# Conditioning sums in fixed runs, more load buffers and split row statistics in the first stage of a diffusion backbone kernel

## The chip, the core and the metric

The kernel runs on one core of a Trainium2 chip. A core has TensorE (PE in the profile, with its weight loads as PEld), VectorE (DVE), ScalarE (ACT), GpSimd (POOL) and SyncE (SP), and sixteen DMA engines that move data between memory and the on-chip buffers. Every engine works through its own list of instructions in order and waits at semaphores for the others. All loads of this kernel are issued from SP. The metric is the time of one execution on the device, in microseconds (us); a change is measured against runs of the kernel before.

## The reference

Two layers of a diffusion backbone over 256 latent tokens and 256 context tokens of width 2048, all in float32. Only the part that the first stage computes is shown: shift and scale from the conditioning vectors, the normed and modulated tokens, and the first products with the input projection.

```python
def rms_norm(x, g):
    xf = x.astype(jnp.float32)
    y = xf * lax.rsqrt(jnp.mean(xf * xf, axis=-1, keepdims=True) + EPS)
    return (y * g.astype(jnp.float32)).astype(x.dtype)

def modulate(h, shift, scale):
    return h * (1.0 + scale[:, None, :]) + shift[:, None, :]

def ada_mods(cvec, w, b):
    m = jax.nn.silu(cvec) @ w + b
    return jnp.split(m, N_MOD, axis=-1)
...
        sh1, sc1, gt1, sh2, sc2, gt2 = ada_mods(c, w_ada[layer], b_ada[layer])
        hl = modulate(rms_norm(x, g_norm_mix[layer]), sh1, sc1)
        hc = None
        if ctx_read:
            csh1, csc1, cgt1, csh2, csc2, cgt2 = ada_mods(c_ctx_row, w_ada[layer], b_ada[layer])
            hc = modulate(rms_norm(ctx_s, g_norm_mix[layer]), csh1, csc1)
        if layer % 2 == 0:
            e = layer // 2
            yl, yc = even_mixer(hl, hc, w_in_even[e], w_out_even[e], lbs[0, e], lbs[1, e], g_hgrn_out[e],
                                w_spatial[e], b_spatial[e], g_spatial_v[e], ctx_out_needed)
```

After the mixer (gated linear attention heads beside chunk MLP heads, an output projection, a residual) each layer has a squared-ReLU MLP; layer 1 has a pooling mixer. The change leaves all of that as it is.

## The kernel before, in words

Weights come as raw float32 chunks of up to 1 MB into two buffers of tag raw (`load_w`, lines 172 to 188), and are cut into two parts that TensorE multiplies fast: hi by a cast on ScalarE (line 183), lo by a subtraction on VectorE (line 184), each in three buffers. Tokens are cut in the same way into `xt`.

The first stage is `startup`. It loads the 256 latent and 256 context rows as four blocks of 128 rows (`xraw`), takes the sum of squares of each block in four pieces on ScalarE (line 460), makes all four row factors in one GpSimd instruction (`rstd`, line 289), and scales the blocks by eight VectorE instructions (line 467). Then it goes through nine slices of features, two of one tile of 128 features (numbers 0 and 1) and seven of two tiles (2 to 8). For each slice it

- sums the conditioning weights over all 2048 features (`cond`, lines 477 to 491): tiles `sraw` of 512 KB, two for each of the slice's `2 * nk` pieces, four buffers of tag a4 in all, are multiplied as plain float32 with the conditioning vectors (`cst`, 32 columns) into `ps_as`. Feature tile kt goes to column group kt mod 4 of TensorE, so four tiles in a row use the four groups. A matmul of plain float32 leaves two records in the profile, so one `sraw` tile of a two-tile slice shows as x4;
- copies the sums to `sp`, adds up the four groups with small matmuls (`ps_ac`), transposes the tokens (`ps_t`), applies scale and shift and cuts the result (`modulate`);
- multiplies the tokens with its rows of two weights: `values` (`mmi`, two calls, summed in `v`) and `forgets` (`mmf`, three calls for three heads, summed in `fbacc`).

`cond` and `modulate` of slice i + 1 are written between the five calls of slice i. A scheduler with priorities and its own clock sets the order on each engine, and where two lists are ready it may interleave them; `issue_after` forces an instruction behind another.

After the stage come eight attention heads with the remaining input projections. There and in what follows VectorE also sums up the other conditioning vectors in the background (`ada_task`, lines 295 to 321): 320 tiles `araw` of 512 KB, one multiply-add each (line 310), in the same four a4 buffers, of which one holds the running sum `acc`.

Of the kernel before, what the change touches and what calls it, by code (L numbers as in the profile page):

```python
# [12 lines left out]
F32 = mybir.dt.float32  # L13
# [6 lines left out]
P = 128  # L20
D = 2048
KT = D // P
T = 256
# [12 lines left out]
BATCH = 2  # L36
NG4 = 7
# [3 lines left out]
AT_S = 1  # L41
# [23 lines left out]
def _cols(v):  # L65
    """(..., n * 128) -> (128, ..., n): one value per partition."""
# [84 lines left out]
class Builder:  # L151
    def __init__(self, nc, tc, I, out):
# [4 lines left out]
        self.n_raw = 0  # L157
        self.hold, self.norm = [], None
# [65 lines left out]
    def group_a(self, chunks, lhs, blocks=(0, 1), cols=512):  # L224
        """lhs(kt, blk) -> (hi, lo) [128, 128]; returns psum tiles of two blocks each, or of one if narrow."""
# [23 lines left out]
    def rows_out(self, src, c0, lhs, narrow):  # L249
        """K = 2048 and all 2048 columns in groups of 512, the last ones narrow if asked; yields (psum, first column, width)."""  # L250
# [10 lines left out]
    def group_b(self, chunks, xt):  # L261
        """psum[:, n, 0] holds W_hi x_lo, psum[:, n, 1] holds W_hi x_hi + W_lo x_hi."""
# [12 lines left out]
    def sum_b(self, ps, out):  # L275
        """out [128, 2, 256] = the two halves of group_b."""
# [15 lines left out]
    def ada_task(self, task, dst, row):  # L292
        """task: 1024 columns of w_ada; dst: [128, 8] columns, or a list for a broadcast row."""
# [805 lines left out]
```

## Time and profile before

| what | value |
|---|---|
| median of 3 runs | 2315.47 us (2312.16 to 2319.08) |
| the profiled execution, span | 2316.0 us |
| TensorE busy | 2262.3 us (98%) |
| VectorE busy | 1683.7 us (73%) |
| ScalarE busy | 1101.6 us (48%) |
| first stage, to the last slice's first matmul | 201.6 us |
| data moved | 582.72 MB, mean 252 GB/s |

The page of the profile gives busy time by engine, the chain of work that ended last and the costliest groups of instructions. A busy TensorE is not one at its best: a matmul that keeps only part of the array at work counts as busy as well. So the stages are read one by one from a table of windows, and inside a window from the instructions in order of time. The waits of an engine name who released it last.

### The profile page before, as it was taken

Reading aid. Unit: us, or ns where it says so; the run is one execution under the profiler, and the core shown is the slowest. Engines: PE = TensorE matmul, PEld = TensorE weight load, DVE = VectorE, ACT = ScalarE, POOL = GpSimd, SP = SyncE. Lnnn points to the kernel's source line nnn. Section 1 sums busy time; section 2 is a strip of 40 time slices with the busy share of each in tenths; the row PEclk is TensorE's granted clock in tenths of the full one; section 3 lists DMA queues with packets and bytes.
Section 4 is the critical chain, followed back from the end, with each engine's and each line's share of the span. In section 5 each row is a group of like instructions: output and inputs, shape, how many; then the busy total and the mean of one; then the engine's idle time right before and its main releaser. Section 6 shows DMA issues by size and latency. Waiting matters only on the chain.

```text
span 2316.0 us, 31681 instructions
## 1 busy us (share of the span) xinstructions
PE 2262.3 (98%) x12486; PEld 1855.1 (80%) x12486; DVE 1683.7 (73%) x2038; ACT 1101.6 (48%) x1493; POOL 34.6 (1%) x43
## 2 busy tenths in 40 slices
PE   6999999999999999999999999999999999999998
PEld 3557778778878888888887888888888888888887
DVE  3447989898878766777879888859875555656655
ACT  4224546464535544553554554545444443443443
POOL 0000000001000000000000000000000000000000
PEclk9999999999999999999999999999999999999999
DMA  8576676777878777888878888755875555555553
GB/s 300 213 271 236 220 263 246 252 257 285 300 289 291 283 282 258 291 303 309 302 289 318 308 318 308 264 177 210 294 283 209 186 196 190 185 188 191 191 183 126
DMA packets 111357, 582.72 MB, mean 252 GB/s; under 512 B 13012, under 2 KB 13140, under 8 KB 67304
## 3 DMA queue, kind: packets, MB, share of 16 engines
q1 hardware_dynamic: 111208, 580.70, 69.7%
q8 instruction: 98, 1.61, 0.3%
q14 instruction: 51, 0.42, 0.0%
HBM read 578.55 MB, written 2.10 MB: 251 GB/s over the span
## 4 chain that ended last, share of the span: by engine, by line
PE 80%; DVE 7%; DMA 6%; issue 5%; ACT 2%; POOL 0%; DVEq 0%; SPq 0%; POOLq 0%; ACTq 0%
PE mma L220 34%; PE mmb L220 32%; PE mmf L220 4%; DMA araw<-in_wada 4%; PE mmn L220 3%; PE ps_as L220 2%; PE mmi L220 2%; DVE acc L310 2%; DVE lo L184 2%; ACT hi L183 1%; DMA raw<-in_w_out 1%; PE ps_ada L220 1%; DVE kk L700 0%; PE ps_t L220 0%; ACT junk L460 0%
## 5 line engine op out<-in xcount | busy, mean ns | idle before, releaser
L183 ACT CAST hi<-raw 128x1024 fp32r<-128x1024 f32 (+1 forms) x701 | 731.9, 1046 | 931.7 <-PE mma L220 430.3
L184 DVE TENSOR_TENSOR lo<-raw,hi 128x1024 fp32r<-128x1024 f32 (+1 forms) x701 | 848.2, 1214 | 381.4 <-ACT hi L183 380.1
L220 PE MATMUL mma<-hi,xt 128*128 128x512 f32 x2800 | 872.5, 390 | 0.1
L220 PE MATMUL mmb<-xt,hi 128*128 128x512 f32 x2304 | 814.6, 398 | 1.1 <-DVE xt L388 0.8
L220 PE MATMUL mmb<-xt,lo 128*128 128x256 f32 x2304 | 647.9, 281 | 1.8 <-DVE lo L184 1.8
L220 PEld LDWEIGHTS mma<-hi,xt 128*128 128x128 f32 x2800 | 524.7, 188 | 111.8 <-issue 0.6
L220 PE MATMUL mma<-lo,xt 128*128 128x512 f32 x1400 | 547.2, 391 | 3.6 <-DVE lo L184 3.6
L220 PEld LDWEIGHTS mmb<-xt,hi 128*128 128x128 f32 x2304 | 432.7, 188 | 105.9 <-DVE xt L388 1.0
L310 DVE SCALAR_TENSOR_TENSOR acc<-araw,csil,acc 128x1024 f32<-128x1024 f32 x320 | 409.5, 1280 | 91.7 <-DMA araw<-in_wada 90.3
L220 PEld LDWEIGHTS mmb<-xt,lo 128*128 128x128 f32 x2304 | 435.3, 189 | 4.7 <-DVE lo L184 2.7
L220 PEld LDWEIGHTS mma<-lo,xt 128*128 128x128 f32 x1400 | 262.9, 188 | 62.6 <-DVE lo L184 7.3
L220 PE MATMUL mmf<-xt,hi 128*128 128x512 f32 x512 | 164.6, 394 | 0.0
L220 PEld LDWEIGHTS mmf<-xt,hi 128*128 128x128 f32 x512 | 95.6, 188 | 26.7 <-issue 7.1
L220 PE MATMUL mmf<-xt,lo 128*128 128x512 f32 x256 | 101.0, 395 | 0.0
L220 PE MATMUL mmn<-hi,xt 128*128 128x256 f32 x416 | 76.0, 283 | 0.0
L220 PE MATMUL ps_as<-sraw,cst 128*32 128x512 f32 (+1 forms) x288 | 58.2, 600 | 18.0 <-DMA sraw<-in_wada_h 17.8
L220 PEld LDWEIGHTS mmn<-hi,xt 128*128 128x128 f32 x416 | 65.2, 192 | 0.4
L220 PEld LDWEIGHTS mmf<-xt,lo 128*128 128x128 f32 x256 | 48.1, 188 | 14.5 <-issue 5.0
L220 PE MATMUL mmn<-lo,xt 128*128 128x256 f32 x208 | 58.8, 283 | 0.0
L540 DVE TENSOR_TENSOR v<-mmi,v 128x1024 f32<-128x1024 f32 x16 | 19.6, 1223 | 50.5 <-PE mmi L220 50.5
L388 DVE TENSOR_TENSOR xt<-hup,xt 128x512 fp32r<-128x512 f32 x64 | 43.9, 686 | 12.2 <-ACT xt L387 12.2
L220 PE MATMUL mmi<-hi,xt 128*128 128x512 f32 x128 | 48.4, 432 | 2.5 <-ACT xt L518 2.4
(178 smaller groups left out, 1318.6 us busy)
## 6 DMA issues: line engine op xcount, KB each, us to landing
araw<-in_wada SPq DMA_DIRECT2D x320, 512.0 KB
raw<-in_w_up SPq DMA_DIRECT2D x128, 1024.0 KB
raw<-in_w_down SPq DMA_DIRECT2D x128, 1024.0 KB
sraw<-in_wada_s SPq DMA_DIRECT2D x56, 512.0 KB
raw<-in_w_out SPq DMA_DIRECT2D x16, 1024.0 KB
raw<-in_w_pool SPq DMA_DIRECT2D x16, 1024.0 KB
raw<-in_w_fb SPq DMA_DIRECT2D x10, 1024.0 KB
raw<-in_w_q SPq DMA_DIRECT2D x8, 1024.0 KB
```

The costliest lines, as they stand in the source:

```text
L183: nc.scalar.copy(hi, raw[:, o:o + w])
L184: nc.vector.tensor_sub(lo, raw[:, o:o + w], hi.bitcast(F32))
L220: self.first_mm = self.nc.tensor.matmul(out, lhsT, rhs, start=start, stop=stop, **kw).ins
L310: nc.vector.scalar_tensor_tensor(acc, raw, self.csil[:, c, 0:1], acc, ALU.mult, ALU.add)
L388: return self.nc.vector.tensor_sub(x[:, :, lo], src, x[:, :, hi].bitcast(F32))
L540: nc.vector.tensor_add(dst, ps, dst)
```

## The change

`cond` is called twice for a slice, each time for half of its pieces: four `sraw` tiles in a two-tile slice, two in a one-tile slice. The last tile is multiplied first, and all other matmuls of the run are tied behind that one. The five calls of a slice and the pieces of the next one are tied in a fixed order: values 0, cond run 0, values 1, cond run 1, forgets 0, modulate, forgets 1 and 2. The tag a4 has seven buffers instead of four, for the background's `araw` too, and `sraw` has two more of its own (tag s4, in a pool that lives only as long as `startup`). [...] Squares and scaling of blocks 1 and 3 go to VectorE, those of 0 and 2 stay with or go to ScalarE; each block gets a row factor of its own. Comments were taken out too, so line numbers differ.

```diff
+NA4 = 7
+NS4 = 2
...
-AT_S = 1
...
-        stat = self.tp.tile([P, 4], F32, tag="st4", bufs=1, name="stat4")
+
+        r4 = [self.tp.tile([P, 1], F32, tag="r4", bufs=4, name="r4") for _ in range(4)]
         for b in range(4):
...
-                nc.scalar.activation(junk, xs[b][j // 2][:, 512 * (j % 2):512 * (j % 2) + 512], AF.Square, accum_out=acc2[:, j:j + 1])
-            nc.vector.tensor_reduce(stat[:, b:b + 1], acc2, AX.X, ALU.add)
-        nc.vector.tensor_scalar(stat, stat, 1.0 / D, EPS, ALU.mult, ALU.add)
-        r4 = self.tp.tile([P, 4], F32, tag="r4", bufs=1, name="r4")
-        self.rstd(stat, r4, 4)
-        for b in range(4):
-            for z in xs[b]:
-                nc.vector.tensor_scalar(z, z, r4[:, b:b + 1], None, ALU.mult)
+                z = xs[b][j // 2][:, 512 * (j % 2):512 * (j % 2) + 512]
+                if b % 2:
+                    nc.vector.scalar_tensor_tensor(junk, z, 1.0, z, ALU.mult, ALU.mult, accum_out=acc2[:, j:j + 1])
+                else:
+                    nc.scalar.activation(junk, z, AF.Square, accum_out=acc2[:, j:j + 1])
+            ms = self.tp.tile([P, 1], F32, tag="ms4", bufs=4, name="ms4")
+            nc.vector.tensor_reduce(ms, acc2, AX.X, ALU.add)
+            nc.vector.tensor_scalar(ms, ms, 1.0 / D, EPS, ALU.mult, ALU.add)
+            self.rstd(ms, r4[b], 1)
+        for j in range(2):
+            for b in range(4):
+                z = xs[b][j]
+                if b % 2:
+                    nc.vector.tensor_scalar(z, z, r4[b], None, ALU.mult)
+                else:
+                    nc.scalar.activation(z, z, AF.Copy, scale=r4[b])
...
-        def cond(i, c):
+        def cond(i, run):
...
+            for c in range(run * nk, run * nk + nk):
+                src = I["wada_h"][2 * k0 + c] if nk == 1 else I["wada_s"][2 * k0 - 4 + c]
+                for h in range(2):
+                    self.n_sraw += 1
+                    if self.n_sraw % (NA4 + NS4) < NS4:
+                        t = self.sp.tile([P, 1024], F32, tag="s4", bufs=NS4, name="sraw")
+                    else:
+                        t = self.ap.tile([P, 1024], F32, tag="a4", bufs=NA4, name="sraw")
+                    nc.sync.dma_start(t, src[:, 1024 * h:1024 * h + 1024])
+                    todo += [(n * c + j, t, j * w % 1024) for j in range(n) if j * w // 1024 == h]
+            first = None
+            for kt, t, at in todo[::-1]:
...
+                with self.tc.issue_after(first) if first is not None else nullcontext():
+                    m = self.mm(st["psa"][32 * g:32 * g + 32, 0:w], cst[:, kt, :], t[:, at:at + w], start, run == 1 and kt < n * nk + 4, skip_group_check=True)
+                first = first if first is not None else m
...
+            steps = [lambda: values(i, 0, wi[0])] + more * [lambda: cond(i + 1, 0)] + [lambda: values(i, 1, wi[0])]
+            steps += more * [lambda: cond(i + 1, 1)] + [lambda: forgets(i, 0, wf)] + more * [lambda: modulate_first(i + 1)]
+            steps += [lambda h=h: forgets(i, h, wf) for h in range(1, N_START)]
+            for fn in steps:
+                with self.tc.issue_after(st["last"]) if "last" in st else nullcontext():
+                    fn()
+                st["last"] = self.first_mm
...
-    nc = bacc.Bacc("TRN2", target_bir_lowering=False, num_devices=1)
+    nc = bacc.Bacc("TRN2", target_bir_lowering=False, num_devices=1, dynamic_dma_scratch_size=1024)
```

TensorE, where slice 3's values are multiplied (`mmi<-hi,xt_96`), in the kernel before; `ps_as x2` is one `sraw` tile for slice 4:

```order
L220 MATMUL ps_as<-sraw,cst 32x512 x2
L220 MATMUL mmi<-hi,xt_96 128x512
L220 MATMUL mmi<-lo,xt_96 128x512
L220 MATMUL mmi<-hi,xt_96 128x512
L220 MATMUL ps_as<-sraw,cst 32x512 x2
L220 MATMUL mmi<-hi,xt_96 128x512
L220 MATMUL mmi<-lo,xt_96 128x512
L220 MATMUL mmi<-hi,xt_96 128x512 x2
```

The same place in the changed kernel, from the end of values 0 on:

```order
L222 MATMUL mmi<-hi,xt_96 128x512
L222 MATMUL ps_as<-sraw,cst 32x512 x8
L222 MATMUL mmi<-hi,xt_96 128x512
L222 MATMUL mmi<-lo,xt_96 128x512
L222 MATMUL mmi<-hi,xt_96 128x512 x2
```

The tiles of slice 4 no longer stand one by one between single matmuls; the four of a run are together, and a second run of x8 stands behind values 1.

ScalarE, from the end of slice 1 to slice 2, in the kernel before (`xt1` holds the tokens of slice 2, `hi<-raw 128x1024` and `128x512` the weights):

```order
L495 COPY sp_425<-ps_as_360 128x512
L183 CAST hi_466<-raw_464 128x1024
L515 ACTIVATE mtmp_441<-ps_t_436,mcol_432 128x256
L518 CAST xt1_95<-mtmp_441 128x512
L183 CAST hi_472<-raw_470 128x1024
L183 CAST hi_476<-raw_470 128x512
L515 ACTIVATE mtmp_451<-ps_t_446,mcol_432 128x256
L518 CAST xt1_95<-mtmp_451 128x512
```

The same place in the changed kernel, with the last copies of slice 0's `forgets` and slice 1's tokens `xt0` ahead:

```order
L575 COPY fbacc_198<-mmf_344 128x1024
L538 ACTIVATE mtmp_339<-ps_t_334,mcol_330 128x256
L575 COPY fbacc_199<-mmf_352 128x1024
L541 CAST xt0_94<-mtmp_339 128x512
L185 CAST hi_478<-raw_476 128x1024
L518 COPY sp_429<-ps_as_380 128x512
L185 CAST hi_484<-raw_482 128x1024
L185 CAST hi_488<-raw_482 128x512
L538 ACTIVATE mtmp_445<-ps_t_440,mcol_436 128x256
L541 CAST xt1_95<-mtmp_445 128x512
```

Both casts of the `forgets` weights of slice 2 now stand ahead of the first `mtmp` of slice 2; and the third copy of slice 0 stands ahead of the cast of slice 1's tokens.

VectorE, around the start of slice 8 (`xt7` holds its tokens), in the kernel before:

```order
L519 TENSOR_TENSOR xt7_101<-mtmp_1335,xt7_101 128x2x256
L519 TENSOR_TENSOR xt7_101<-mtmp_1345,xt7_101 128x2x256
L310 SCALAR_TENSOR_TENSOR acc_1475<-araw_1478,csil_78,acc_1475 128x1024
L554 TENSOR_TENSOR fbacc_186<-mmf_1305,fbacc_186 128x1024
L184 TENSOR_TENSOR lo_1373<-raw_1370,hi_1372 128x1024
L184 TENSOR_TENSOR lo_1377<-raw_1370,hi_1376 128x512
L554 TENSOR_TENSOR fbacc_187<-mmf_1350,fbacc_187 128x1024
```

The same place in the changed kernel:

```order
L312 SCALAR_TENSOR_TENSOR acc_1491<-araw_1497,csil_78,acc_1491 128x1024
L526 TENSOR_TENSOR mcol_1324<-ps_ac_1319,bcol_213 128x4 x2
L577 TENSOR_TENSOR fbacc_197<-mmf_1303,fbacc_197 128x1024
L527 SCALAR_TENSOR_TENSOR mcol_1324<-mcol_1324,gcol_215 128x4
L312 SCALAR_TENSOR_TENSOR acc_1491<-araw_1500,csil_78,acc_1491 128x1024
L540 TENSOR_SCALAR mtmp_1333<-ps_t_1328,mcol_1324 128x256
L540 TENSOR_SCALAR mtmp_1343<-ps_t_1338,mcol_1324 128x256
L577 TENSOR_TENSOR fbacc_198<-mmf_1348,fbacc_198 128x1024
L542 TENSOR_TENSOR xt7_101<-mtmp_1333,xt7_101 128x2x256
L542 TENSOR_TENSOR xt7_101<-mtmp_1343,xt7_101 128x2x256
L312 SCALAR_TENSOR_TENSOR acc_1491<-araw_1545,csil_78,acc_1491 128x1024
```

The first tiles of the background (`acc<-araw`) moved up: three of them now stand ahead of slice 8's tokens, where none stood. Counted from there on, about four more of them stand ahead of a given weight cut than before all through the heads.

## Rows read from the trace of the kernel before

**Rows 1.** Page: busy time, share of the span and instructions of each engine.

```profile
PE 2262.3 (98%) x12486; PEld 1855.1 (80%) x12486; DVE 1683.7 (73%) x2038; ACT 1101.6 (48%) x1493; POOL 34.6 (1%) x43
```

**Rows 2.** Windows: length, busy PE, PEld, DVE, ACT, POOL; granted clock, DMA share, GB/s.

```profile
0.00:27.76 27.76, 7.31 (x49) 2.61 (x49) 9.80 (x28) 15.66 (x41) 2.33 (x11) 1.00 0.92 337
...
40.95:58.98 18.03, 16.29 (x75) 7.77 (x71) 8.54 (x12) 3.13 (x6) 0.00 (x0) 1.00 0.86 305
58.98:85.76 26.78, 26.78 (x109) 14.06 (x109) 11.35 (x17) 7.13 (x11) 0.00 (x0) 0.94 0.58 207
85.76:110.72 24.96, 24.96 (x109) 13.51 (x108) 12.00 (x17) 5.26 (x8) 0.00 (x0) 1.00 0.61 222
110.72:134.49 23.77, 23.77 (x109) 13.46 (x108) 11.50 (x16) 5.26 (x8) 0.00 (x0) 1.00 0.69 254
134.49:156.80 22.31, 22.31 (x110) 13.59 (x109) 11.58 (x16) 5.36 (x8) 0.00 (x0) 1.00 0.68 248
...
179.12:201.60 22.48, 22.30 (x109) 13.77 (x109) 12.59 (x17) 5.31 (x8) 0.95 (x1) 1.00 0.68 251
201.60:560.00 358.40, 343.95 (x2582) 278.41 (x2581) 325.16 (x618) 202.72 (x379) 10.33 (x8) 1.00 0.70 251
```

**Rows 3.** PE in order of time, three places: start, duration, instruction [wait before].

```profile
39.63 0.39 PE L220 MATMUL mmf<-xt,hi 128*128 128x512 f32 x1
39.95 1.07 PE L220 MATMUL ps_as<-sraw,cst 128*32 128x512 f32 x8
...
41.28 0.39 PE L220 MATMUL mmi<-lo,xt 128*128 128x512 f32 x1
...
85.44 0.39 PE L220 MATMUL mmf<-xt,hi 128*128 128x512 f32 x1
85.76 1.05 PE L220 MATMUL ps_as<-sraw,cst 128*32 128x512 f32 x4
...
87.08 0.39 PE L220 MATMUL mmi<-lo,xt 128*128 128x512 f32 x1
87.31 0.40 PE L220 MATMUL mmi<-hi,xt 128*128 128x512 f32 x1
...
178.80 0.39 PE L220 MATMUL mmf<-xt,hi 128*128 128x512 f32 x1
179.12 1.92 PE L220 MATMUL ps_as<-sraw,cst 128*32 128x512 f32 x16
...
181.31 0.40 PE L220 MATMUL mmi<-lo,xt 128*128 128x512 f32 x1
```

**Rows 4.** SP's waits, 0 to 201.6 us: total, times, longest.

```profile
SPq L485 <- PE ps_as L220: 115.3, 47, 9.4
```

**Rows 5.** Windows as in rows 2: a slow stretch, and a fast one for DMA.

```profile
60.00:64.00 4.00, 4.00 (x12) 1.68 (x10) 2.33 (x3) 1.48 (x3) 0.00 (x0) 0.64 0.00 0
...
1250.00:1300.00 50.00, 50.00 (x255) 41.28 (x254) 44.87 (x42) 22.52 (x26) 0.95 (x1) 1.00 0.89 321
```

**Rows 6.** The head in order of time: DVE's scaling, PE's last load wait.

```profile
17.80 5.39 DVE L467 TENSOR_SCALAR xraw<-xraw,r 128x1024 f32<-128x1024 f32 x8 [1.22 <-POOL r L289]
...
21.04 1.08 PE L220 MATMUL ps_as<-sraw,cst 128*32 128x256 f32 x8 [0.15 <-DMA sraw<-in_wada_h]
```

**Rows 7.** ACT and PE in order of time at the ends of slices 0 and 1.

```profile
40.30 1.02 ACT L552 COPY fbacc<-mmf 128x1024 f32<-128x1024 f32 x1
...
58.83 1.56 ACT L183 CAST hi<-raw 128x1024 fp32r<-128x1024 f32 x2
...
58.98 0.50 PE L220 MATMUL mmi<-hi,xt 128*128 128x512 f32 x1 [1.49 <-ACT xt L518]
```

**Rows 8.** DVE in order of time around the start of slice 8.

```profile
198.68 1.28 DVE L310 SCALAR_TENSOR_TENSOR acc<-araw,csil,acc 128x1024 f32<-128x1024 f32 x1
...
203.27 1.22 DVE L554 TENSOR_TENSOR fbacc<-mmf,fbacc 128x1024 f32<-128x1024 f32 x1
```

**Rows 9.** DVE's waits, 201.6 to 560 us: total, times, longest.

```profile
DVE acc L310 <- DMA araw<-in_wada: 15.7, 12, 3.0
```

More of the change, by code (lines that the diff above doesn't have):

```diff
@@ L297, in first @@
         def first():
-            st["acc"] = self.ap.tile([P, 1024], F32, tag="a4", bufs=4, name="acc")
+            st["acc"] = self.ap.tile([P, 1024], F32, tag="a4", bufs=NA4, name="acc")
             nc.gpsimd.memset(st["acc"], 0.0)
@@ L304, in chunk @@
                 first()
-            raw = self.ap.tile([P, 1024], F32, tag="a4", bufs=4, name="araw")
+            raw = self.ap.tile([P, 1024], F32, tag="a4", bufs=NA4, name="araw")
             nc.sync.dma_start(raw, self.I["wada"][task * 16 + c])
@@ L314, in last @@
         def last():
-            hi, lo = (self.ap.tile([P, 1024], F32R, tag="a4", bufs=4, name="apart") for _ in range(2))
+            hi, lo = (self.ap.tile([P, 1024], F32R, tag="a4", bufs=NA4, name="apart") for _ in range(2))
             nc.scalar.copy(hi, st["acc"])
@@ L474, in startup @@
         slices = [(0, 1), (1, 1)] + [(k, 2) for k in range(2, KT, 2)]
-        def cond(i, c):
+        def cond(i, run):
             k0, nk = slices[i]
-            n_c, w = 2 * nk, 256 * nk
-            if c == 0:
-                st["psa"] = self.pa.tile([P, 512], F32, tag="ax", name="ps_as")
-            src = I["wada_h"][2 * k0 + c] if nk == 1 else I["wada_s"][2 * k0 - 4 + c]
-            raws = [self.ap.tile([P, 1024], F32, tag="a4", bufs=4, name="sraw") for _ in range(2)]
-            for h in range(2):
-                nc.sync.dma_start(raws[h], src[:, 1024 * h:1024 * h + 1024])
-            n = 2048 // w
-            for j in range(n):
-                at = j * w % 1024
-                g, kt = j % 4, n * c + j
-                self.mm(st["psa"][32 * g:32 * g + 32, 0:w], cst[:, kt, :], raws[j * w // 1024][:, at:at + w], kt < 4, kt >= KT - 4, skip_group_check=True)
+            w = 256 * nk
+            n = 2048 // w
+            if run == 0:
+                st["psa"], st["seen"] = self.pa.tile([P, 512], F32, tag="ax", name="ps_as"), set()
+            todo = []
+            for c in range(run * nk, run * nk + nk):
[10 more added lines that the diff above has]
+            for kt, t, at in todo[::-1]:
+                g = kt % 4
+                start = g not in st["seen"]
+                st["seen"].add(g)
+                with self.tc.issue_after(first) if first is not None else nullcontext():
+                    m = self.mm(st["psa"][32 * g:32 * g + 32, 0:w], cst[:, kt, :], t[:, at:at + w], start, run == 1 and kt < n * nk + 4, skip_group_check=True)
+                first = first if first is not None else m
         def modulate(i):
@@ L565, in startup @@
             wf = self.load_w(I["w_fbs"][k0 // 2, :, n * j:n * (j + nk)], n * nk)
-            ahead = []
-            if i + 1 < len(slices):
-                ahead = [lambda c=c: cond(i + 1, c) for c in range(2 * slices[i + 1][1])] + [lambda: modulate_first(i + 1)]
-            todo = [lambda w=w: values(i, w, wi[0]) for w in range(2)] + [lambda h=h: forgets(i, h, wf) for h in range(N_START)]
-            for q, fn in enumerate(todo):
-                if ahead and q == len(todo) - AT_S:
-                    ahead.pop()()
-                elif q < 2:
-                    for _ in range((len(ahead) - 1) // (2 - q)):
-                        ahead.pop(0)()
-                fn()
+            more = i + 1 < len(slices)
+            steps = [lambda: values(i, 0, wi[0])] + more * [lambda: cond(i + 1, 0)] + [lambda: values(i, 1, wi[0])]
[5 more added lines that the diff above has]
+                st["last"] = self.first_mm
         return fbacc
@@ L805, in gmlp_u, with mixer_even @@
         self.split(4 + pair, 2, 3, u)
-    def mixer_even(self):
+    def mixer_even(self, fbacc):
         nc, I = self.nc, self.I
-        fbacc, fbs = self.startup(), {}
+        fbs = {}
         self.plan(LEFT_H, LOADS_H)
@@ L1054, in build @@
             self.NG4, self.NT2 = NG4, NT2
[L1055 removed]
+            with pool(name="tp0", bufs=1) as self.tp, pool(name="vp", bufs=1) as self.vp:
                 self.ada(1, c["sh2_0"])
@@ L1065, in build @@
                 gate2 = self.ada(9, None)
-                self.mixer_even()
-                stat = self.out_proj()
+                with pool(name="sp", bufs=1) as self.sp:
+                    fbacc = self.startup()
+                with pool(name="gp", bufs=1) as self.gp:
+                    self.mixer_even(fbacc)
+                    stat = self.out_proj()
             with pool(name="gates", bufs=4) as self.gate_pool:
```

4 lines of the change are left out of this document (2 added, 2 removed).

## The prediction

> **What bounds the kernel now.** I read the busy times first: TensorE is busy 98% of the span [rows 1], so whatever makes the kernel shorter must either make TensorE's own work shorter or fill its idle 54 us. Next I read the table of windows, cut at the slices of the first stage [rows 2]. The reader should see three things. In the first 27.76 us TensorE does little and DMA moves 337 GB/s: the head is loading. From 58.98 us on TensorE has no idle time, yet slices 2 to 5, which do the same work, take 26.78, 24.96, 23.77 and 22.31 us; slices 6 and 7 are like 5. So busy TensorE time differs in length, and DMA is used to 58 to 69% only. In the heads (201.6 to 560 us) TensorE idles 358.40 - 343.95 = 14.45 us and VectorE is busy 91%.
>
> Why the slices differ is in the instructions in order of time [rows 3]. An undisturbed matmul starts 0.23 us after the last (87.08 to 87.31). Where a single `sraw` tile stands between two matmuls (x4), the second matmul behind it starts 87.08 - 85.44 = 1.64 us after the one ahead, instead of 2 x 0.23: the tile costs **1.18 us**. Two tiles together (x8) cost 41.28 - 39.63 - 0.46 = **1.19 us**, no more than one, since they fill all four column groups where one fills two. Four tiles (x16) cost 181.31 - 178.80 - 0.46 = **2.05 us**. In TensorE's order slices 2 and 3 have eight single tiles (8 x 1.18 = 9.44 us), slices 1 and 4 one x8 and six singles (8.27), slices 5 to 7 one x16 and four singles (6.77). This accounts for the table: slice 3 less slice 5 should be 2.67 and is 2.65 us, slice 4 less slice 5 should be 1.50 and is 1.46.
>
> **Runs of four tiles.** After the change each slice from 1 to 7 has two x16: 4.10 us, and nothing stands inside them. Slices 2 and 3 gain 5.34 us each, slice 4 4.17, slices 5 to 7 2.67 each: 22.9 us together, and a slice should take 22.31 - 2.67 = 19.6 us. Slice 1 gains 4.17 too. [...]
>
> [...]
>
> **Loads.** A waiting run holds up TensorE, as the run now starts with its last tile. Today SP waits 115.3 us in the stage for TensorE to free an `sraw` buffer [rows 4]; with nine buffers the next slice's tiles can be issued one slice ahead, right after the run that frees them. A slice moves eight tiles of 512 KB, 512 KB and 768 KB of weights, 5.5 MB. In 19.6 us that is 280 GB/s; the best stretch later in the trace keeps 321 GB/s [rows 5], the head 337 [rows 2], by which 5.5 MB need 17.1 us. So some 2.5 us of each slice are spare and I charge nothing. What stands in SP's list ahead of the tiles is the `forgets` weight load, which waits for a raw buffer until its predecessor has been cut, early in a slice; what it holds up is needed a slice later. If this cover is gone, the loads set the pace: a rival below. Slices 1 and 2 have the least reserve, since all nine buffers must first be filled behind the head; a wait of 0 to 3 us may fall there.
>
> **The order on ScalarE between slices 0, 1 and 2** is worse. Today slice 2's first matmul waits 1.49 us for its tokens on ScalarE [rows 7], of 18.03 - 16.29 = 1.74 us idle in slice 1 [rows 2]. Afterwards both casts of the `forgets` weights (1.56 us, [rows 7]) stand ahead of these tokens, and the second can only start when slice 1's last matmul has freed its buffer. I take 1.49 + 1.56, some 3.0 us, which is 1.3 more than now; bounds 0 and 3 more than now. At the end of slice 0 the third copy (1.02 us, [rows 7]) now stands between the last `forgets` and the cast of slice 1's tokens, where nothing waits today: 1.02 plus the cast and its way, bounded by the 1.49 of the other place, 1.0 to 2.5; I take 2.0. [...]
>
> **Row statistics.** Today the squares run on ScalarE alone and scaling takes VectorE 5.39 us, until 23.19 us [rows 6]. In halves, with a row factor per block, I see the scaling end up to 2 us earlier, worked out from VectorE's list: it waits for block 0's squares, does block 1's (four pieces, half of a 1.28 us operation each), waits for GpSimd, and the same again for blocks 2 and 3. But slice 0's sums wait for loads: the last tile comes at 21.04 us [rows 6], and afterwards a run starts with it, so that up to 1.08 us of matmuls move behind it; ScalarE also casts a weight before it copies the sums. I take 0; bounds -1.5 and +1.5.
>
> **Slice 8.** VectorE now has three background operations ahead of slice 8's tokens and a fourth behind them (its order is shown above), where one stood in all. At 1.28 us each [rows 8] the sum `fbacc`, for whose buffer `values` 1 of slice 8 waits, which began at 203.27, 1.67 us after the slice [rows 8], comes up to 3.8 us later. Some of that is in VectorE's spare time: +2.5 us, bounds 0 and 4.
>
> **The heads.** The background has seven buffers, so its tiles land earlier. VectorE waits 15.7 us for them in the heads [rows 9] and TensorE idles 14.45 us there [rows 2]. Only some of these idle times follow such a wait, and the scheduler puts about four background operations earlier, ahead of work that TensorE waits for. I take -2 us; bounds -12 (nearly all idle time gone) and +8 (an operation of 1.28 us ahead of a wait in six of the eight heads). Behind 560 us nothing is charged: TensorE has few gaps there, and VectorE has room for work that comes earlier. [...]
>
> **The sum.** -22.9 (slices 2 to 7), -4.2 + 1.3 (slice 1), -0.5 + 2.0 (slice 0), 0 (head), +2.5 (slice 8), -2 (heads): -23.8 us. The profiled execution has a span of 2316.0 us, 0.5 above the median of the runs; 2315.5 - 23.8 gives **2292 us**. Its own bounds, with the larger terms not all at one end together, are 2283 to 2303.
>
> **The rivals.** (1) Only the number of runs counts. Slices 1 to 7 have 45 runs today and 14 afterwards; a merge saves 2 x 1.19 - 2.05 = 0.33 us, so 31 of them 10.2 instead of 27.1, and the sum is 2309. The equal cost of x4 and x8 speaks against it. 4%. (2) Loads set the pace, at the whole run's mean of about 251 GB/s (the heads' row, [rows 2]), because SP stands still behind the weight load: 5.5 MB take 21.9 us, slices 2 to 7 take 6 x 21.9 and 1.4 for the clock instead of 142.6 us and gain 9.8, not 22.9: 2305. For it: no slice of the stage has moved over 254 GB/s except slice 1 with 305. Against it: SP's 115 us of waiting for buffers explains that. 9%. (3) The deeper background frees the heads: 10 us more than in the sum, 2282. For it the 15.7 us of waits, against it that VectorE stays 91% busy. 9%. (4) **Slower**: the background's operations, now earlier in VectorE's list, stand between the last steps of each of the eight heads, on which TensorE waits. Three of them in each, 8 x 3 x 1.28 = 30.7 us, less the 21.8 gained before the heads: 2324. It decides from the point where VectorE has no spare time left in a head; today it has 33 us in 358. 4%. That the change doesn't do what it says (the scheduler breaks up the runs) is excluded by TensorE's order, where all are whole.
>
> **How the numbers follow.** The forecast has 74%, the rivals 4, 9, 9 and 4%. A measurement of this kernel tells about 0.3% (7 us) from no change. Faster than 2308.5: the forecast, (3) and most of (2), 0.88; within: (1) and the rest of (2), 0.08; slower: 0.04. The range takes the forecast's own bounds and reaches up to (2): 2282 to 2306.
>
> **What would show it.** Right: all `ps_as` in the profile as x16, slices 3 to 7 at 19.6 us with no idle TensorE time, DMA near 280 GB/s there, about 3 us of waiting for tokens ahead of slice 2, and slice 8 starting near 178 us. Wrong: `ps_as` waits for DMA in slices 3 to 7 (rival 2); slices shortened by only 1 to 3 us without such waits (rival 1); idle time in the heads far from 14 us, with `acc` just ahead of it on VectorE (rivals 3, 4).

## The result and the profile after

The changed kernel takes **2281.97 us** (median of 4 runs, 2281.31 to 2284.89) against 2317.27 us of the kernel before on the same chip (median of 4, 2312.16 to 2326.20). The ratio is 0.9854 with a 95% interval of 0.9828 to 0.9881: 35.3 us faster by the medians, where 24 were forecast. The profiled executions have spans of 2279.4 and 2316.0 us, 36.6 us apart.

The busy line of the page of the changed kernel, and its row for the conditioning matmuls (busy time and mean ns of one, then the idle time ahead and what ended it):

```profile
PE 2229.7 (98%) x12486; PEld 1857.4 (81%) x12486; DVE 1685.3 (74%) x2053; ACT 1104.3 (48%) x1481; POOL 36.6 (2%) x46
L222 PE MATMUL ps_as<-sraw,cst 128*32 128x512 f32 (+1 forms) x288 | 34.6, 604 | 18.6 <-DMA sraw<-in_wada_h 18.6
```

TensorE has the same 12486 instructions as in [rows 1] and is busy 32.6 us less, 23.6 of them in this row (58.2 us in the kernel before). Its only wait of `ps_as` for loads, 18.6 us, lies in the head.

The windows of the changed kernel cut at its slices 0 to 8, columns as in [rows 2]; the ninth line is slice 8 up to the first matmul of the first head, the last one from there to the norm of the first FFN layer:

```profile
26.81:41.05 14.24, 12.62 (x70) 8.03 (x70) 3.09 (x8) 7.48 (x10) 0.00 (x0) 1.00 1.01 365
41.05:57.74 16.69, 14.86 (x78) 8.36 (x78) 9.54 (x14) 4.29 (x6) 0.00 (x0) 0.90 0.85 292
57.74:80.11 22.37, 21.31 (x108) 14.68 (x109) 10.93 (x17) 5.94 (x9) 0.00 (x0) 0.92 0.80 285
80.11:99.68 19.57, 19.57 (x109) 13.66 (x108) 11.48 (x16) 5.38 (x8) 0.00 (x0) 1.00 0.76 283
...
138.83:158.40 19.57, 19.57 (x109) 13.67 (x108) 11.48 (x16) 5.38 (x8) 0.95 (x1) 1.00 0.74 258
158.40:177.98 19.58, 19.58 (x110) 13.66 (x108) 14.92 (x19) 5.27 (x8) 0.00 (x0) 1.00 0.82 304
177.98:193.06 15.08, 13.94 (x62) 11.19 (x60) 14.71 (x14) 6.03 (x6) 0.00 (x0) 1.00 0.68 250
...
193.06:686.07 493.01, 484.99 (x3373) 400.83 (x3372) 441.12 (x754) 271.57 (x468) 16.53 (x12) 1.00 0.75 273
```

Slices 3 to 7 take 19.57 or 19.58 us each without idle TensorE time, where 24.96, 23.77 and 22.31 us stood in [rows 2]. Slices 1 and 2 have idle time and a granted clock of 0.90 and 0.92. The same last stretch in the kernel before:

```profile
215.57:721.79 506.22, 488.67 (x3373) 400.11 (x3372) 445.60 (x757) 270.64 (x468) 16.46 (x12) 1.00 0.74 267
```

So the first stage, up to the first matmul of the first head, ends 215.57 - 193.06 = 22.5 us earlier, and the next 500 us are 506.22 - 493.01 = 13.2 us shorter. Of these, TensorE's idle time is 17.55 - 8.02 = 9.5 us; the other 3.7 us are time of the matmuls themselves, spread over many groups, and no run shows their cause. Everything after that takes 1593.3 us for 1594.2. VectorE's waits for background tiles in this stretch (total, times, longest), before and after:

```profile
DVE acc L310 <- DMA araw<-in_wada: 19.7, 16, 3.0
```

```profile
DVE acc L312 <- DMA araw<-in_wada: 4.6, 6, 1.2
```

TensorE in order of time in the changed kernel (start, duration, instruction, the wait ahead of it): a run in slice 3, the waits ahead of slices 1 and 2, and the wait in slice 8.

```profile
41.05 0.50 PE L222 MATMUL mmi<-hi,xt 128*128 128x512 f32 x1 [1.62 <-ACT xt L541]
43.68 2.72 PE L222 MATMUL ps_as<-sraw,cst 128*32 128x512 f32 x16
...
57.74 0.50 PE L222 MATMUL mmi<-hi,xt 128*128 128x512 f32 x1 [1.83 <-DVE mtmp L540]
59.53 1.22 PE L222 MATMUL mmi<-hi,xt 128*128 128x512 f32 x2 [1.06 <-DVE xt L542]
...
82.60 0.39 PE L222 MATMUL mmi<-hi,xt 128*128 128x512 f32 x1
82.92 1.93 PE L222 MATMUL ps_as<-sraw,cst 128*32 128x512 f32 x16
84.78 0.50 PE L222 MATMUL mmi<-hi,xt 128*128 128x512 f32 x1
85.11 0.39 PE L222 MATMUL mmi<-lo,xt 128*128 128x512 f32 x1
...
182.00 0.50 PE L222 MATMUL mmi<-hi,xt 128*128 128x512 f32 x1 [1.15 <-DVE fbacc L577]
```

From the matmul ahead of the run to the second one behind it are 85.11 - 82.60 = 2.51 us, 2.05 more than two undisturbed ones: the price of the x16 in [rows 3]. At 43.68 a run takes 2.72 us, at a lowered clock (0.61 granted from 43 to 46 us).

### The profile page after: what moved, and what is told of

Read it like the earlier page. It is cut to its first block, busy times and chain, and to the rows that moved or that the text cites. A ratio compares the mean times of both kernels' runs of the same rounds, so it can differ in the third digit from the quotient of the medians.

```text
span 2279.4 us, 31572 instructions
## 1 busy us (share of the span) xinstructions
PE 2229.7 (98%) x12486; PEld 1857.4 (81%) x12486; DVE 1685.3 (74%) x2053; ACT 1104.3 (48%) x1481; POOL 36.6 (2%) x46
## 4 chain that ended last, share of the span: by engine, by line
PE 87%; DVE 6%; ACT 2%; issue 2%; DMA 2%; POOL 0%; SPq 0%; POOLq 0%; DVEq 0%; ACTq 0%
PE mma L222 37%; PE mmb L222 34%; PE mmf L222 5%; PE mmn L222 3%; PE mmi L222 2%; DVE lo L186 2%; DVE acc L312 1%; PE ps_as L222 1%; DMA araw<-in_wada 1%; ACT hi L185 1%; DMA sraw<-in_wada_h 1%; PE ps_ada L222 1%; DVE kk L721 1%; PE ps_o L222 1%; DVE qg L721 0%
## 5 line engine op out<-in xcount | busy, mean ns | idle before, releaser
L222 PE MATMUL ps_as<-sraw,cst 128*32 128x512 f32 (+1 forms) x288 | 34.6, 604 | 18.6 <-DMA sraw<-in_wada_h 18.6
L703 ACT COPY both<-kk 128x256 f32<-128x256 f32 x64 | 26.4, 413 | 50.5 <-DVE kk L721 41.5
```

The source lines that it names most:

```text
L222: self.first_mm = self.nc.tensor.matmul(out, lhsT, rhs, start=start, stop=stop, **kw).ins
L703: nc.scalar.copy(o.rearrange("p (s j i) -> p j s i", j=2, i=hh), bass.AP(src.tensor, src.offset, [list(src.ap[0]), [st + hh, 2], [seg, ns] ...
```

## The experiments

Three things were to be told apart: whether the runs of four or the nine load buffers made the stage shorter; whether a lone tile pays for idle column groups or for the two ends of a run; and where the 13 us behind the stage come from.

### Background buffers: four instead of seven

The first stage keeps nine buffers; behind it the background has four, as in the kernel before.

```diff
-NA4 = 7
-NS4 = 2
+NA4 = 4
+NS4 = 5
```

> The changed kernel with the nine load buffers of the first stage split as five and four instead of two and seven: the stage itself is as in the changed kernel, but the background behind it has four buffers again, as before. Theory (the some 13 us gained behind the stage come from the deeper background): slice 8 still starts near 178 us, VectorE waits for araw loads behind it some 15 us again, and the time is about 2295 us (2282 + 13). Rival (the gain behind the stage comes from the earlier start or the other order, not from the buffers): 2282 us, within 3.

2294.05 us (2291.21 to 2297.52), ratio 0.9906 (0.9885 to 0.9927). The theory holds: 12.1 us are lost. The stretch from the first head's first matmul to the FFN norm, in the same columns:

```profile
194.46:700.95 506.49, 488.93 (x3373) 402.71 (x3372) 443.68 (x755) 271.07 (x468) 16.17 (x12) 0.99 0.74 264
```

It is 506.49 us long again, with 17.56 us of idle TensorE time, as in the kernel before. The six other kernels below that have seven background buffers loaded from SP take 492.4 to 496.2 us for it, whatever else differs. One of the waits with four buffers can be followed through three engines of this kernel, in order of time:

```profile
415.63 1.28 DVE L312 SCALAR_TENSOR_TENSOR acc<-araw,csil,acc 128x1024 f32<-128x1024 f32 x1 [4.04 <-DMA araw<-in_wada]
...
418.90 0.85 DVE L742 TENSOR_REDUCE sd<-md 128x64 f32<-128x384 f32 x1
```

```profile
419.84 0.24 ACT L745 COPY st<-sd 32x64 f32<-32x64 f32 x1 [2.50 <-DVE sd L742]
```

```profile
421.86 0.49 PE L222 MATMUL ps_o<-v,st 128*128 128x128 f32 x2 [1.69 <-ACT st L745]
```

VectorE stands 4.04 us on a background tile that hasn't landed. The head's own sum `sd` stands behind it in VectorE's order, ScalarE waits 2.50 us for that, and TensorE 1.69 us for ScalarE. A late load of something that nobody needs yet has reached TensorE. The kernel before has the same chain twice: behind VectorE's waits of 2.60 us (until 331.50) and 2.40 us (until 403.12), TensorE waits 2.01 and 1.60 us for `st`.

### Five and six buffers

The same edit with 5 and 4, and with 6 and 3.

> The changed kernel with the nine load buffers split as four for the first stage alone and five that the background keeps. With four kept buffers the time was 2294 us, with seven 2282. Theory (each araw buffer lets the load start one operation of the background earlier, and a load of 512 KB takes longer than three operations of 1.28 us when it shares the engines with the weights): the waits for araw behind the stage fall by about half and the time is near 2288 us. Rival (one more buffer already covers the load): 2282. Rival (only the full seven do): 2294.

> The changed kernel with the nine load buffers split as three for the first stage alone and six that the background keeps. Theory (each buffer more covers a part of the load): near 2284 us. Rival (saturated): 2282 as with seven.

Five: 2297.06 us (2296.58 to 2300.08), ratio 0.9927 (0.9911 to 0.9942); six: 2286.40 us (2285.18 to 2287.62), ratio 0.9878 (0.9863 to 0.9893). The stretch is 507.3 us with five and 500.3 with six, between 506.5 (four) and 493.0 (seven). So the gain is not in equal steps: the fifth buffer gives nothing, the sixth about 7 us of the stretch and the seventh as much again. My 2288 for five was wrong. With five the waits for `araw` between 178 and 722 us are shorter than with four (12.1 against 19.3 us) and the time isn't, so their sum alone doesn't set it. Part of the difference is the clock. The kernels with four, five and six buffers each have one wait of TensorE of 3.4 to 3.6 us in the heads, and from the first head's first matmul to about 520 us the granted clock reads 0.99 on the mean there. Here with five, the wait and two windows around and behind it:

```profile
376.03 0.66 PE L222 MATMUL ps_sc<-both 128*32 128x64 f32 x16 [3.43 <-ACT both L703]
```

```profile
375.00:379.00 4.00, 2.97 (x39) 2.64 (x40) 4.00 (x10) 4.00 (x9) 0.95 (x1) 0.50 0.01 2
379.00:383.00 4.00, 4.00 (x24) 3.37 (x24) 2.79 (x6) 2.02 (x4) 0.00 (x0) 0.68 0.42 141
```

By these windows it costs 2.97 x 0.5 + 4 x 0.32 = 2.8 us, an estimate. In the heads of the kernels before and changed every 4 us read a granted clock of 1.00. Another part is late weights. In the same stretch ScalarE waits 32.4 us for the loads `raw<-in_w_out` in the kernel before, 30.6 us with four buffers, 27.6 with five, 1.7 with six and 6.8 with seven; the waits of TensorE for `lo` from 656 to 677 us in the kernel before follow such loads. The number of buffers also changes the order in which the scheduler lists the work. How much of the gain is background tiles that come earlier, how much weights that come earlier and how much that order stays open.

### The loads of the background on another queue

The first experiment's kernel, and later the fastest one, with the `araw` loads issued from GpSimd's queue. Both leave the amount of data as it is.

```diff
-            nc.sync.dma_start(raw, self.I["wada"][task * 16 + c])
+            nc.gpsimd.dma_start(raw, self.I["wada"][task * 16 + c])
```

> The kernel of the first experiment (four background buffers, 2294 us) with the loads of the background (araw) issued on GpSimd's queue instead of SP's. An araw load that waits for a buffer then holds up no weight load behind it. Theory (with few buffers the araw loads hold up the weight loads in SP's list, and TensorE waits for what is cut from those): the waits of TensorE for lo and hi behind the stage go, and the time falls from 2294 to about 2284 us although the araw loads wait for buffers as long as before. Rival (VectorE's own waits for late araw tiles, and the order they force, are the cause): 2294 us, with DVE waits for araw as in the first experiment.

> The fastest kernel so far (seven background buffers, tokens earlier, statistics of before, 2277 us) with the araw loads on GpSimd's queue. Theory (SP's list is the cause): what is left of it behind the stage goes as well, 2 to 4 us, 2274 us. Rival (it is not): 2277 us, or more if loads through GpSimd cost VectorE time.

2344.61 us (ratio 1.0134, 1.0111 to 1.0157) and 2354.46 us (ratio 1.0170, 1.0146 to 1.0194): both far slower, which neither theory expected. So SP's list can't be tested this way, since the new queue brings the tiles later still: VectorE waits 173.2 us for them with four buffers (105.2 with SP's queue), and 116.7 with seven (66.3). Why they come later was not taken apart. Each issue takes GpSimd 0.53 us; and both kernels keep `dynamic_dma_scratch_size=1024`, which I had set with all loads issued from SP; whether it plays a part was not tested. But the second of these kernels shows the same mechanism at its plainest. VectorE and TensorE in the first FFN layer, in order of time:

```profile
830.90 1.28 DVE L312 SCALAR_TENSOR_TENSOR acc<-araw,csil,acc 128x1024 f32<-128x1024 f32 x1 [3.93 <-DMA araw<-in_wada]
832.10 1.22 DVE L186 TENSOR_TENSOR lo<-raw,hi 128x1024 fp32r<-128x1024 f32 x1
```

```profile
833.38 0.50 PE L222 MATMUL mma<-lo,xt 128*128 128x512 f32 x1 [3.33 <-DVE lo L186]
```

The wait of 3.93 us for a background tile stands directly ahead of the cut `lo` of a weight, and 3.33 us of it reach TensorE. The first FFN layer takes 1490.55 - 692.01 = 798.5 us there, instead of 731.8 to 736.4 in all kernels with loads from SP alone (748.0 in the first of these two).

### Nine buffers without the runs

The kernel before with nine load buffers (seven of them for the background), but its own order of the tiles and its own row statistics.

```diff
-            raws = [self.ap.tile([P, 1024], F32, tag="a4", bufs=4, name="sraw") for _ in range(2)]
+            raws = []
+            for _ in range(2):
+                self.n_sraw += 1
+                if self.n_sraw % (NA4 + NS4) < NS4:
+                    raws.append(self.sp.tile([P, 1024], F32, tag="s4", bufs=NS4, name="sraw"))
+                else:
+                    raws.append(self.ap.tile([P, 1024], F32, tag="a4", bufs=NA4, name="sraw"))
```

> The kernel before with the changed kernel's nine load buffers and its seven for the background, but with the conditioning tiles of slices 1 to 7 still multiplied between the other matmuls as their loads are issued, and with the row statistics of before. Theory (the runs of four made the gain of the stage, the buffers that behind it): slices 2 and 3 stay near 25 to 27 us, slice 8 starts some 17 us or more later than in the changed kernel, and the time is about 2297 to 2303 us. Rival (more buffers alone make the gain, since the tiles were only late): slices of 20 us and 2282 us.

2300.45 us (2299.92 to 2302.57), ratio 0.9932 (0.9911 to 0.9954), within the theory's range. Slices 2 and 5 of this kernel:

```profile
59.23:87.00 27.77, 27.77 (x113) 14.20 (x113) 12.33 (x18) 7.75 (x12) 0.00 (x0) 0.94 0.64 218
...
136.60:157.67 21.07, 21.07 (x113) 13.54 (x109) 11.48 (x16) 5.37 (x8) 0.00 (x0) 1.00 0.72 262
```

From the start of slice 1 to that of slice 8 the kernel before takes 160.65 us, this one 153.69, the changed kernel 136.93. So the buffers alone are worth 7.0 us there, since the scheduler bunches more tiles in the later slices, and the runs with their fixed order 16.8 more. In the later slices the rival came true: slice 6 takes 19.58 us here without fixed runs, as in the changed kernel; slices 2 to 4, with 27.77, 24.97 and 24.63 us, gain nothing. The stretch behind the stage takes 496.2 us, near the changed kernel's 493.0: that gain comes with the buffers, without the runs.

### The runs with four buffers

> The changed kernel with its runs of four, but only four load buffers in the first stage and four for the background. Theory (runs need tiles loaded a slice ahead): with four buffers a run's tiles can be issued only when the run before has been multiplied, 3 us before the next run begins; 2 MB at 321 GB/s take 6.5 us and the way some 2, so each of seven slices loses about 5.5 us, 38 together, and with the 13 of the background the time is about 2333 us, slower than before. Rival (the buffers of the stage do not matter): slices of 19.6 us and about 2295 us.

Here `NA4 = 4` and `NS4 = 0`. 2349.35 us (2346.11 to 2353.02), ratio 1.0145 (1.0122 to 1.0168): runs without the buffers are slower than the kernel before. Two runs in slice 1, and windows around the second:

```profile
44.89 3.19 PE L222 MATMUL ps_as<-sraw,cst 128*32 128x512 f32 x16
...
56.04 3.64 PE L222 MATMUL ps_as<-sraw,cst 128*32 128x512 f32 x16 [6.38 <-DMA sraw<-in_wada_s]
```

```profile
52.00:57.00 5.00, 0.96 (x8) 0.30 (x12) 0.06 (x1) 0.00 (x0) 0.00 (x0) 0.73 0.78 292
57.00:60.00 3.00, 3.00 (x17) 0.68 (x10) 0.00 (x0) 0.22 (x1) 0.00 (x0) 0.50 0.29 98
60.00:64.00 4.00, 4.00 (x25) 3.49 (x25) 1.85 (x5) 0.36 (x1) 0.00 (x0) 0.86 0.94 292
```

TensorE waits 37.1 us for `sraw` tiles in seven waits; 38 were expected. The 2 us for the way were an estimate: the first load of the kernel before, 1 MB, takes 5.03 us, and 1 MB at the 337 GB/s of the head [rows 2] takes 3.1. No run shows this term alone; here the first run of slice 1 ends at 48.08 us and the second starts at 56.04, 7.96 us later, where the expectation has 6.5 + 2. The 16 us beyond the forecast are by an estimate mostly the clock: after the wait of 6.38 us it is granted at 0.50 for 3 us and at 0.86 on the mean of the next 4, which costs 3 x 0.5 + 4 x 0.14 = 2.1 us. After the next wait, of 5.26 us, it is at 0.50 over 80 to 84 us and at 0.87 over 84 to 88, by the same sum 2.5 us. Seven slices at 2.1 to 2.5 us give 14 to 18 us. From 30 to 178 us the granted clock reads 0.87 on the mean in this kernel and 0.98 in the changed one.

### The column groups

Two kernels keep the runs, their number and their loads, and change only which column groups their matmuls use. One sorts a run so that the matmuls of one group follow each other. The other puts the second run of each slice into two column groups (slices 1, 3, 5, 7) or one (0, 2, 4, 6).

```diff
+            todo.sort(key=lambda z: (z[0] % 4, z[0]))
```

```diff
-                g = kt % 4
+                g = kt % 4 if run == 0 else kt % (2, 1)[i % 2]
```

> The changed kernel with the sixteen matmuls of each run in the order of their column group, four of one group behind each other, instead of the four groups in turn. Theory (idle column groups are what a lone tile pays for): a run of sixteen then takes about 4.6 us instead of 2.05, which is 36 us for the fourteen runs, and 2318 us in all. [...]

> The changed kernel with the second run of every slice in fewer column groups: the second run of slices 1, 3, 5 and 7 in two groups, that of slices 0, 2, 4 and 6 in one; the first run of each slice stays in four. The number of runs, of matmuls and of loads is that of the changed kernel. Theory (matmuls of different column groups run side by side, and a lone tile pays for the groups that it leaves idle): from one instruction per group in 1.19 us and two in 2.05 a further one in a group costs 0.86, so a run in two groups takes 1.19 + 3 x 0.86 = 3.8 us, one in a single group 1.19 + 7 x 0.86 = 7.2, and the time is 4 x 1.7 + 3 x 5.2 and some 2 for the narrow run of slice 0, 24 us more: 2306. Rival (only the two ends of a run cost): all runs stay at 2.05 us and the time at 2282.

The sorted order: 2280.69 us (2278.80 to 2282.86), ratio 0.9848 (0.9829 to 0.9868), no change; its runs take 1.94 to 1.95 us instead of 1.92. By my expectation this spoke against the column groups. (It counted the records of the profile: a run has eight matmuls, two of each group, not sixteen.) Fewer groups: 2306.36 us (2305.01 to 2306.75), ratio 0.9953 (0.9936 to 0.9971), against 2306 expected. Three runs of that kernel, the first and second of slice 2 and the second of slice 3, the second ones with a matmul ahead and the second matmul behind:

```profile
66.13 1.92 PE L222 MATMUL ps_as<-sraw,cst 128*32 128x512 f32 x16
...
70.61 0.39 PE L222 MATMUL mmi<-hi,xt 128*128 128x512 f32 x1
70.93 7.05 PE L222 MATMUL ps_as<-sraw,cst 128*32 128x512 f32 x16
...
78.25 0.40 PE L222 MATMUL mmf<-xt,lo 128*128 128x512 f32 x1
...
95.27 0.39 PE L222 MATMUL mmi<-hi,xt 128*128 128x512 f32 x1
95.59 3.63 PE L222 MATMUL ps_as<-sraw,cst 128*32 128x512 f32 x16
...
99.48 0.40 PE L222 MATMUL mmf<-xt,lo 128*128 128x512 f32 x1
```

An x16 is eight matmul instructions: two for each group with four groups, four with two, eight with one. The times 1.92, 3.63 and 7.05 us lie on a line: (3.63 - 1.92) / 2 = (7.05 - 3.63) / 4 = 0.855 us for each instruction in a group. Priced as in [rows 3], by the starts of the matmuls around them, they cost 2.05, 99.48 - 95.27 - 0.46 = 3.75 and 78.25 - 70.61 - 0.46 = 7.18 us, which leaves 0.34 us for a run as such, whatever its length. So the groups do work side by side, and a lone tile's 1.18 us are 0.855 for a round in which groups stand idle and some 0.33 for the run as such. The error in my first expectation was that TensorE keeps strictly to the order of the groups: a run of eight instructions takes 1.94 to 1.95 us sorted by group and 1.92 with the groups in turn, so a second matmul of one group doesn't hold up the other groups' matmuls listed behind it. A round saved is worth 0.855 us here, a run saved 0.34 us; what the 0.34 us consist of is not shown.

### Row statistics and ScalarE's order

Three kernels: the changed one with the row statistics of before; the changed one with the next slice's tokens made ahead of the first `forgets` group in the one-tile slices 0 and 1; and both together.

```diff
-            steps += more * [lambda: cond(i + 1, 1)] + [lambda: forgets(i, 0, wf)] + more * [lambda: modulate_first(i + 1)]
+            steps += more * [lambda: cond(i + 1, 1)]
+            early = nk == 1
+            steps += (not early) * [lambda: forgets(i, 0, wf)] + more * [lambda: modulate_first(i + 1)] + early * [lambda: forgets(i, 0, wf)]
```

> The changed kernel with the row statistics and the scaling of before (squares on ScalarE, scaling on VectorE). Theory (the split of the statistics ends the scaling earlier, and the 0.95 us by which slice 0 starts earlier are its): slice 0 starts at 27.8 us instead of 26.8 and the time is about 2283 us. Rival (the loads of the head decide): slice 0 starts at 26.8 us and the time is 2282.

> The changed kernel with the tokens of the next slice made ahead of the first forgets group in the two narrow slices 0 and 1, so that ScalarE has the token casts in its list ahead of the casts of the forgets weights. Theory (the waits of 1.62, 1.83 and 1.06 us ahead of slices 1 and 2 are ScalarE's order): they go, and with them the two stretches at the lower clock behind them, 1.4 us each; 4.5 + 2.8 = 7 us, 2275 us. Rival (what is late next, the sums of the runs or the forgets weights, takes their place): waits of the same length under another name, and 2282 us.

> The kernel with the tokens made earlier in slices 0 and 1 (2278.8 us), with the row statistics of before. With the changed kernel's order the statistics of before cost nothing, since the 1.6 us by which slice 0 then began later came back in a stretch that stayed at the full clock. Theory (without that stretch in either, the split statistics are worth the time by which slice 0 starts earlier): slice 0 starts about 1 us later and the time is 2280 us. Rival (the loads of the head set the start either way): 2279.

The statistics of before: 2280.85 us (2280.18 to 2283.56), ratio 0.9850 (0.9832 to 0.9867), no difference to the changed kernel. Slice 0 does start later, at 28.45 us for 26.81. Not all of this is the statistics'. The last run ahead of slice 0 waits for a load, here in the changed kernel and with the statistics of before:

```profile
20.53 1.93 PE L222 MATMUL ps_as<-sraw,cst 128*32 128x256 f32 x16 [1.29 <-DMA sraw<-in_wada_h]
```

```profile
21.12 1.94 PE L222 MATMUL ps_as<-sraw,cst 128*32 128x256 f32 x16 [1.62 <-DMA sraw<-in_wada_h]
```

In the changed kernel slice 0 starts 6.28 us after this run, and so it does in the kernels with four and five background buffers and with the tokens earlier (6.27 to 6.28), where the load lands between 20.84 and 21.81 us. With the statistics of before it starts 7.33 us after it. So the split is worth 1.05 us in this pair, and the other 0.59 are a load that landed earlier, which differs from kernel to kernel. On the other side slice 1 keeps the full clock (1.00 granted from 40 to 48 us) and takes 57.66 - 42.53 = 15.13 us instead of 16.69, so that slice 2 starts at 57.66 us, for 57.74 in the changed kernel. TensorE ahead of slice 1 in this kernel:

```profile
42.53 0.50 PE L222 MATMUL mmi<-hi,xt 128*128 128x512 f32 x1 [1.62 <-ACT xt L533]
44.38 1.92 PE L222 MATMUL ps_as<-sraw,cst 128*32 128x512 f32 x16
```

The wait of 1.62 us is the same, the run behind it takes 1.92 us and not 2.72. What the changed kernel gains in the head, the clock (0.61) takes back in slice 1. That isn't due to the statistics: with five and six background buffers, the statistics split and a wait of 1.63 us, slice 1 takes 15.13 us too, and with four buffers 16.72. What decides it stays open.

Tokens earlier: 2278.78 us (2277.08 to 2279.77), ratio 0.9834 (0.9817 to 0.9852). Both together: 2276.99 us (2275.65 to 2280.11), ratio 0.9835 (0.9820 to 0.9849). With the tokens earlier alone the granted clock reads 1.00 from 27 to 178 us; in both, the runs of slice 1 take 1.92 us, and in slices 0 and 1 waits of 0.9 us or less each, 2.6 us together, stand in place of the 4.5 (the rival's other names, but shorter). From the start of slice 0 to the first head's first matmul the kernel with the tokens earlier takes 188.82 - 28.09 = 160.73 us instead of 166.25, so 5.5 us go, where 7 were expected. Its slice 0 starts 1.3 us later, as its load lands later (21.81 us), and in the medians 2 to 3 us are to be seen. With both together slice 0 starts at 28.25 us for 28.09 and the time is no longer: the rival, by which the loads set the start, holds there. These two are the fastest kernels of the study, but their intervals overlap with the changed kernel's, and the 2 to 5 us are not secured.

## Why the prediction was right, and where it was not

The forecast was 2292 us with a range of 2282 to 2306; the time, 2281.97 us, lies at its very edge. The steps ahead of the heads sum up to -21.8 us in the forecast and to -22.5 measured; the heads alone missed by 11 us, as much as lies between the forecast and that edge, so that the range held is luck. By the profiled spans, step by step:

| step | forecast us | measured us | from |
|---|---|---|---|
| runs of four, slices 2 to 7 | -22.9 | -22.4 | 142.62 to 120.24 |
| slice 1 | -2.9 | -1.3 | 18.03 to 16.69 |
| slice 0 | +1.5 | +1.1 | 13.19 to 14.24 |
| head | 0 | -1.0 | 27.76 to 26.81 |
| slice 8 | +2.5 | +1.1 | 13.97 to 15.08 |
| heads, and the stretch behind 560 us to the FFN norm | -2 | -13.2 | 506.22 to 493.01 |
| the rest | 0 | -0.9 | 1594.2 to 1593.3 |

**The runs** are right in size and in cause. Slices 3 to 7 take the 19.6 us that [rows 3] gave, at 258 to 306 GB/s and with no wait for a tile, so the loads don't set the pace (rival 2). That idle column groups are the larger price and not the number of runs alone (rival 1) is shown by the kernel with fewer groups: its number of runs is the same and it loses 24 us. But the rival's part is in the sum as well. By the prices above, slices 1 to 7 go from 45 runs to 14, 31 x 0.34 = 10.5 us, and from 48 rounds to 28, 20 x 0.855 = 17.1 us; together 27.6, for the 22.9 + 4.2 of the forecast.

**The order on ScalarE** gave waits of the size that was forecast: 1.83 + 1.06 = 2.9 us for slice 2's tokens for 3.0, and 1.62 us ahead of slice 1 for 2.0. Of the two casts that were added up for the first, only the shorter one stood in the gap, as it waited for slice 1's last matmul to free its buffer:

```profile
50.41 1.05 ACT L185 CAST hi<-raw 128x1024 fp32r<-128x1024 f32 x1
55.95 0.62 ACT L185 CAST hi<-raw 128x512 fp32r<-128x512 f32 x1 [4.48 <-PE mmf L222]
```

The rest of the gap is the steps from `ps_t` to the two token tiles behind it. So the step was right in kind, and its 1.56 us for both casts right in sum by luck. A stretch at a lowered clock also came in slice 1, 0.61 granted from 43 to 46 us, where the kernel before has 1.00; the sum has no term for it, and by the kernels with 15.13 us for this slice it cost 16.69 - 15.13 = 1.6 us. The 1.4 us that rival (2) and the expectation for the tokens made earlier count for such a stretch are 4 x (1 - 0.64), from the slow stretch in [rows 5].

**Slices 0 and 1** need to be read together. The x8 for slice 2 stood at 39.95 us, ahead of slice 1's first matmul [rows 3], so slice 1's window lost 6 x 1.18 - 4.10 = 3.0 us of conditioning matmuls and not 4.17, and the other 1.19 went from the window of slice 0; and of the 2.9 us of waits 1.06 lie in slice 2's. That slice 1 would stand at -2.9 without the clock, as forecast, is these two errors cancelling. Over slices 0 to 7 the windows give -22.6 us where -24.3 were forecast, and the 1.6 of the clock are nearly all of the difference. The head's -1.0 is smaller than what the landing of its last load alone moves from kernel to kernel (20.53 to 21.81 us). No run shows the 0.5 us that the sum takes off for slice 0's runs of 256 columns: by the records four x8 of 1.08, 1.08, 0.64 and 0.64 us (25.74 to 34.92 us in the kernel before, the first of them in the head) became two x16 of 1.94 and 1.07 us, 0.43 us less.

**The heads** are the step that failed. I charged -2 us there and nothing behind 560 us; the stretch gave 13. The mechanism was among the rivals (3), with the right price of 10 us more and the right time of 2282, but only 9%. What I set against it was that VectorE stays 91% busy. It is 93% busy now (342.35 of 366.94 us up to 560 us), and TensorE's idle time in the stretch has halved all the same. The busy share was the wrong row to ask: a wait of VectorE for `araw` costs what stands behind it in its order, and the list of waits [rows 9] with the instructions behind each would have shown that for the two chains named above, 3.6 us of TensorE's waits. TensorE's waits from the first head's first matmul to the FFN norm in the changed kernel (total, times, longest), all that are over 0.2 us in sum:

```profile
PE ps_sc L222 <- ACT both L703: 3.8, 6, 1.3
PE ps_mx L222 <- DVE vg L806: 2.5, 2, 1.6
PE ps_o L222 <- ACT st L745: 0.9, 4, 0.3
```

and the first of the same list in the kernel before:

```profile
PE ps_o L220 <- ACT st L724: 4.6, 5, 2.0
PE mma L220 <- DVE lo L184: 3.1, 5, 0.8
PE ps_ada L334 <- ACT crow L332: 2.9, 1, 2.9
PE ps_sc L220 <- ACT both L682: 2.9, 6, 1.1
PE ps_sd L220 <- ACT both L682: 1.9, 1, 1.9
```

`mma<-lo`, `ps_ada` and `ps_sd` are gone, and `ps_o` fell by 3.7 us; `ps_mx` and `ps_sc` grew by 2.1 and 0.9. Only two of the waits for `ps_o` directly follow a wait of VectorE for `araw` in the kernel before; why `ps_ada` and `ps_sd` went is not shown. Of the waits for `mma<-lo`, 2.5 us lay behind 540 us, where I had charged nothing because TensorE had few gaps; from there to the norm it had 3.5 us of them, and now has 2.5. That the buffers are the cause of the 13 us is shown by the kernel with four; by which ways is shown only in part.

**Slice 8** cost 1.1 us, not 2.5: the wait for `fbacc` is 1.15 us. The slower rival (4), background work ahead of the heads' last steps, didn't occur.

## What to carry to other kernels

Price a matmul that uses part of TensorE's columns by the round it takes (0.855 us here) and by its run as such (0.34 us): gather such matmuls until every column group has work, make the runs long, and give the runs enough buffers that a whole run is loaded ahead, since the same runs with four buffers were slower than no runs at all. When a low-priority stream shares an in-order engine with the critical work, look at what stands behind each of its waits and not at the engine's busy share; a deeper buffer for it was worth 13 us here, beside the 22 of the runs.

## What the runs showed of the hardware that was not expected

- Within a run, the order of the column groups makes no difference (1.92 and 1.95 us), though the groups' number does (1.92, 3.63, 7.05 us).
- The same wait of 1.62 to 1.63 us ahead of slice 1 was followed by a run of 2.72 us in the changed kernel (0.61 granted from 43 to 46 us) and of 3.29 us with four background buffers, and by one of 1.92 us with the statistics of before (1.00 granted there) and with five or six buffers.
- At the start of slice 0 of the changed kernel a matmul starts 0.43 us after the last (28.68 to 29.11 us), later 0.23 us, though the granted clock reads 1.00 in the whole window.
- DMA moved 365 GB/s over the 14 us of slice 0, more than the 337 of the head in [rows 2] that the prediction took as the best.
- The same background loads from GpSimd's queue left VectorE waiting 173.2 us for them, and from SP's 105.2 us, with four buffers each.
